# Softmax sums of a head pair inverted once per pair and multiplied into the pair's gate; masks made three tiles ahead; W_out fetched into free stream rows

## The chip, the cores and the metric

The kernel runs on one core of one Trainium2 chip. The metric is the device time of a whole execution in microseconds (us). TensorE (PE) does the matmuls, VectorE (DVE), ScalarE (ACT) and GpSimd (POOL) the rest; SyncE (SP) issues nearly all DMAs from one queue, in the order in which they stand in its program. PEld is PE's weight load, which overlaps its matmuls.

## The reference, cut to what matters

Two layers over 1024 tokens of width 1024. The change is in layer 1, whose main branch is forgetting attention (16 heads of 64 dimensions, shared keys and values, causal, with a cumulative log forget gate):

```python
logits = einsum('bqhd,bkhd->bhqk', qi, k) * scale + (cum[t] - cum[s])
p = softmax(where(kpos <= qpos, logits, -inf))
y_main = einsum('bhqk,bkhd->bqhd', p, v)
y = concatenate([y_main * silu(g_main), y_mem * silu(g_mem)])
x = layer_norm(alpha * x + y @ w_out)
```

A row of `p` is exp(..)/sum. Dividing the probabilities by the sum before the product with v, or dividing the row of `y_main` after it, gives the same. Since `y_main` is multiplied by silu(g_main), the division can also go into that gate.

## The kernel before

All large products run on PE with operands split into a high and a low half (f16 or bf16 with fp32r), so that three half-products give nearly f32 accuracy. A **slab** is a product of one 128-column piece of a weight with the whole X: 48 matmuls of 512 columns (L326). Its weights come in two pieces, each loaded (`split_w`, L210) and split into halves: by ACT (L171) and DVE (L172) before the attention stage, by POOL (L175, L192, L177) within it (`low[0]`).

The stage around the change has three parts.

- **Start** (`start_units`, L954): the values and forget logits of the first four heads (`v_first`, L835; 24 matmuls for each of eight token tiles), the key slab of pair 0 (its weights split early by `own_weights`), its query slab, and the key slab of pair 1. Between them DVE works out the forget gates in a chain of some 25 small operations (L863 to L876), whose result PE needs at L884; the cumulative sums go to DRAM (`cumd`) and come back as rows `R`, spread over the partitions (L985). The weights of the query slab and of the next key slab are split when the slab's own code is reached.
- **Attention** (`fox`, L1116): heads 0 to 15 in pairs; in each head eight query tiles, the longest first (tile 7 has 1024 keys, tile 0 has 128). For one tile, PE makes logits in one or two parts into the PSUM banks `L` (three of them); DVE adds the forget row, or on the last part the mask `C` that POOL made two tiles ahead (L978), and keeps the minimum (L1004); ACT takes exp into the PSUM banks `T` (two of them) and accumulates the sum (L1012). One tile later DVE inverts the sum (L1022 or L1024, then L1025), ACT writes the high half exp times inverse (L1040), and DVE the low half (L1041). A DMA transposes the halves (L1057); six tiles later (`LAG`) PE multiplies them with v (L1066), four tiles at a time, into the one bank `O`. ACT and DVE scale the result into `o` (L1086, L1087): for the long half two tiles after its matmuls. POOL multiplies `o` with the pair's gate (L1100), and a DMA stores it to `y1d`.
- **End** (`OutProj`, L541): W_out comes in 24 pieces of 128x512. The first ones are fetched into `land` buffers and split during pair 7; the rest through the four `raw` buffers, shared with the masks, in the last loop (`hd == HEADS`, six steps) and in `rest` (L612).

PE's order is the order of the code (`manual_schedule`); that of the other engines is set by a scheduler. Between logits and values PE works on slabs of the next pair: `Fill.pump` spreads them over a pair's 16 tiles. Each tile's share is a mean of what is left less its own attention work, so that all tiles get the same PE time; the table `MORE` then adds or takes columns by the tile's place (800 less at the first, 2330 more at the second, 1130 at the third, 1420 less at the last). A column of a 128-row operand is the unit; `VALUES` tells where the values products fall.

Of the kernel before, what the change touches and what calls it, by code (L numbers as in the profile page):

```python
# [18 lines left out]
P = 128  # L19
S = 1024  # L20
# [20 lines left out]
MORE = (-800, 2330, 1130, 410, -310, -70, -1270, -1420)  # L41
# [37 lines left out]
def trunk_kernel(ctx, tc, x, xT, memT, win, wk, wv0, wv, wmk, wmv, wout, poolw, pscale, lng, lnb, bforget, out):  # L79
# [128 lines left out]
    pinned_w = [False]  # L208

    def split_w(src_dram, shape, sc=None, r=None):  # L210
# [3 lines left out]
        if sc is not None:  # L214
            to = half_of(wt, shape)
            if low[0]:
                gp_scaled_hi_lo(to, r, sc)
            else:
                scaled_hi_lo(to, r, sc, tc.keep_in_program_order if pinned_w[0] else lambda ins: ins)
            return to  # L220
# [320 lines left out]
    class OutProj:  # L541
# [8 lines left out]
        def fetch_two(self, land):  # L550

            n = self.n + len(self.raws)
            for j in range(2):
                nc.sync.dma_start(land[:, j, :], wout[self.l, n // 2 % 2, 2 * self.KKS[n // 4] + j])
                self.raws.append(land[:, j, :])
# [56 lines left out]
        def rest(self, resid, X, dst):  # L612
# [14 lines left out]
            for sp, c in order:  # L627
# [5 lines left out]
                if splits:  # L633
                    self.split(splits.pop(0))
# [158 lines left out]
    with tc.tile_pool(name="in1", bufs=1) as in1:  # L793
# [41 lines left out]
        def v_first():  # L835
# [3 lines left out]
            for s in range(ST):  # L839
# [16 lines left out]
                )  # L856

# [52 lines left out]
        own_ws = []  # L910

        def own_weights():
            own_ws.extend(split_w(wk[0, pc], [P, 4, P], sws[1]) for pc in range(2))

        def k_units(p):
# [8 lines left out]
            yield from slab(wk[p] if p else own_ws, X, evac, g=1)  # L924
            pairs[p] = [[(own[:, 0], own[:, 1]), (odd[:, 0], odd[:, 1])]]

        def q_units(p):
# [8 lines left out]
            yield from slab(win[1, p], X, evac, g=1)  # L936
# [17 lines left out]
        def start_units(own, following):  # L954

            pinned_w[0] = True
# [32 lines left out]

# [38 lines left out]
        joined = []  # L1028

        def halves(hd, i, es, r):  # L1030

            L = (i + 1) * P
            if i in (2, 0):
                pair = joined.pop()[:, 2 * L + 2 * P :]
            else:
                pair = sb([P, 2 * S], "P", 4, F16)
                if i in (3, 1):
                    joined.append(pair)
            for lo, up, e in es:
                nc.scalar.activation(pair[:, lo:up], e, AF.Copy, scale=r)  # L1040
                nc.vector.scalar_tensor_tensor(pair[:, L + lo : L + up], e, r, pair[:, lo:up], ALU.mult, ALU.subtract)  # L1041
            return hd, i, pair
# [16 lines left out]
        def values(hd, c, o, gs):  # L1059
# [23 lines left out]

            def out():

                nc.scalar.activation(oc, acc[other, :], AF.Copy, scale=un[own])  # L1086
                nc.vector.scalar_tensor_tensor(oc, acc[own, :], un[own], oc, ALU.mult, ALU.add)  # L1087
                if b:
                    pair_out(hd // 2, c, o, gs.get(hd // 2))

            return out
# [24 lines left out]
        def fox(following, out_proj):  # L1116
            fill, past, fresh = Fill(), [None] * LAG, [None]
            gs, outs = {}, []
# [6 lines left out]
            for i in range(2):  # L1125
                mask(0, ST - 1 - i, ahead_R)
            for hd in range(HEADS + 1):
# [16 lines left out]
                for i in range(ST if hd < HEADS else LAG):  # L1144
# [4 lines left out]
                    if hd < HEADS:  # L1149
# [131 lines left out]
```

## Time and profile before

| | |
|---|---|
| median of 3 runs | 1198.69 us (1197.19 to 1199.53) |
| the profiled execution | 1197.8 us, its span 1196.0 us |
| granted TensorE clock, mean | 0.995 |
| layer 0 and the memory attention of layer 1 | 0 to about 590 us |
| start (v_first, first slabs, forget gates) | about 590 to 650 us |
| attention, 16 heads | about 650 to 1046 us |
| end (last loop, first products with W_out) | about 1046 to 1076 us |
| products with W_out and layer norm | about 1076 to 1196 us |

The span is the time from the first to the last instruction of one execution; 1.8 us of the execution's own time lie around it. A row of the timeline reads: start, duration, engine, line, operation, out<-in, shapes, count, and in brackets the idle time of the engine before it and what ended it.

### The profile page before, as it was taken

How to read it: one execution, taken by the hardware profiler on the slowest of the kernel's cores; microseconds unless marked ns; L12 is line 12 of the kernel's file. 1: busy time of each engine (PE TensorE's matmuls, PEld its weight loads, DVE VectorE, ACT ScalarE, POOL GpSimd, SP SyncE). 2: the span in 40 equal slices, each digit the busy share in tenths (PEclk: the TensorE clock that was granted, in tenths of full speed). 3: DMA queues.
4: the chain of work that ended last, by engine and by line, in shares of the span. 5: the costliest groups of instructions: out<-in, count | busy, mean ns of one | idle time of the engine just before them, and what ended most of it. 6: DMA issues, size and time to landing. Idle time of an engine off the chain costs nothing. (4 is left out here: it accounts for less than half of the span.)

```text
span 1196.0 us, 19806 instructions
## 1 busy us (share of the span) xinstructions
PE 1167.2 (98%) x6941; PEld 672.0 (56%) x6941; DVE 786.4 (66%) x1840; ACT 690.0 (58%) x1520; POOL 279.8 (23%) x429
## 2 busy tenths in 40 slices
PE   8999999999999999999999999999999999989996
PEld 5566776555555556556664555555555555445553
DVE  6744675555765557457644888778777887864654
ACT  6568875976563234466422777667766777675210
POOL 4321001310000000010324454554434331730000
PEclk8999999999999999999999999999999999999999
DMA  7576657754285555355724989979897898795430
GB/s 269 167 236 194 167 107 211 245 178 150 90 296 159 142 141 133 96 150 113 222 83 120 193 170 214 208 175 185 191 196 151 159 177 168 197 253 195 164 118 36
DMA packets 286195, 203.88 MB, mean 170 GB/s; under 512 B 224912, under 2 KB 238352, under 8 KB 286096
## 3 DMA queue, kind: packets, MB, share of 16 engines
q1 hardware_dynamic: 279696, 181.59, 60.5%
q0 software_dynamic: 6400, 21.04, 5.6%
q8 instruction: 54, 0.88, 0.3%
q14 instruction: 45, 0.37, 0.1%
HBM read 116.01 MB, written 22.61 MB: 116 GB/s over the span
## 5 line engine op out<-in xcount | busy, mean ns | idle before, releaser
L356 PE MATMUL pj<-A,w 128*128 128x512 f16 (+2 forms) x2896 | 665.1, 383 | 5.6 <-ACT w L171 2.6
L356 PEld LDWEIGHTS <-w 128*128 128x128 f16 (+1 forms) x2560 | 245.1, 98 | 280.7 <-issue 9.5
L1012 ACT ACTIVATE T<-MK,s 128x512 f32<-128x512 f32 x192 | 111.1, 579 | 62.3 <-DVE s L1004 43.0
L1041 DVE SCALAR_TENSOR_TENSOR P<-T,s,P 128x512 f16<-128x512 f32 x192 | 111.6, 613 | 41.4 <-ACT P L1040 39.1
L1040 ACT ACTIVATE P<-T,s 128x512 f16<-128x512 f32 x192 | 102.9, 576 | 55.9 <-issue 23.4
L175 POOL TENSOR_SCALAR B<-B,scales 128x512 f32<-128x512 f32 x54 | 38.8, 728 | 367.3 <-DMA B<-in_win_dram 343.5
L596 PEld LDWEIGHTS <-T 128*128 128x128 bf16 x736 | 70.6, 98 | 91.8 <-issue 7.6
L978 POOL TENSOR_SCALAR_AFFINE_SELECT raw<-R 128x256 f32<-128x256 f32 (+3 forms) x128 | 60.2, 473 | 146.4 <-DVE s L1025 72.9
L198 DVE TENSOR_TENSOR w<-raw,w 128x512 bf16<-128x512 f32 x76 | 54.3, 714 | 54.2 <-ACT w L197 38.1
L324 PE MATMUL L<-A 128*128 128x512 f16 (+3 forms) x384 | 84.5, 326 | 3.5 <-DVE s L1004 3.5
L356 PEld LDWEIGHTS pj<-A,w 128*128 128x128 f32 x352 | 65.3, 188 | 17.1 <-ACT w L197 1.3
L198 DVE TENSOR_TENSOR T<-T,T 128x1024 bf16<-128x1024 f32 x23 | 28.1, 1220 | 67.2 <-PE pj L596 37.6
L324 PEld LDWEIGHTS <-A 128*128 128x128 f16 x384 | 37.5, 98 | 48.3 <-issue 5.5
L177 POOL TENSOR_TENSOR w<-B,w 128x512 f16<-128x512 f32 x54 | 63.3, 1174 | 2.8
L197 ACT CAST w<-raw 128x512 fp32r<-128x512 f32 x78 | 48.0, 615 | 22.8 <-DMA raw<-in_win_dram 9.7
L197 ACT CAST T<-T 128x1024 fp32r<-128x1024 f32 x23 | 24.1, 1047 | 59.7 <-DMA T<-y1d 31.9
L1066 PEld LDWEIGHTS <-V 128*64 128x64 f16 (+1 forms) x1152 | 50.6, 104 | 13.9 <-issue 6.1
L1066 PE MATMUL O<-T,V 128*64 128x128 f16 (+1 forms) x1152 | 57.5, 220 | 0.5 <-DMA T<-P 0.5
L596 PE MATMUL pj<-B,T 128*128 128x512 bf16 (+1 forms) x192 | 53.2, 385 | 0.0
L199 ACT CAST w<-raw 128x512 bf16<-128x512 f32 x80 | 49.4, 618 | 5.5 <-PE pj L356 4.1
L1004 DVE CUSTOM_DVE_ANT_0 MK<-L,R,scales 128x512 f32<-128x512 f32 x64 | 45.4, 709 | 4.7 <-PE L L324 4.6
L596 PE MATMUL L<-B,T 128*128 128x512 bf16 (+1 forms) x168 | 47.3, 394 | 0.8 <-ACT T L199 0.8
(276 smaller groups left out, 1805.8 us busy)
## 6 DMA issues: line engine op xcount, KB each, us to landing
raw<-in_win_dram SPq DMA_DIRECT2D x66, 256.0 KB, 3.6
W<-in_win_dram POOLq DMA_DIRECT2D x48, 256.0 KB, 4.0
raw<-in_wout_dram SPq DMA_DIRECT2D x40, 256.0 KB, 3.2
R<-cumd SPq DMA_DIRECT2D x16, 512.0 KB, 4.6
B<-in_win_dram SPq DMA_DIRECT2D x15, 512.0 KB, 4.8
y0d<-Y SPq DMA_DIRECT2D x12, 512.0 KB, 4.2
T<-y0d SPq DMA_DIRECT2D x12, 512.0 KB, 4.5
A<-A SPq DMA_DIRECT2D x24, 256.0 KB, 4.4
```

Of the source, the lines that this page charges most:

```text
L177: nc.gpsimd.tensor_tensor(to.lo, src, to.hi, ALU.subtract)
L197: pin(nc.scalar.copy(to.hi, src))
L198: pin(nc.vector.tensor_tensor(to.lo, src, to.hi.bitcast(F32), ALU.subtract))
L199: pin((top or nc.scalar.copy)(to.top, src))
L324: nc.tensor.matmul(acc, a, b, start=i == 0, stop=i == len(terms) - 1)
L356: nc.tensor.matmul(accs[n], a[:, k, :], b[:, pc * 4 + k, n * NH : (n + 1) * NH], start=seen[n] == 1, stop=seen[n] == 3 * KT,)
L596: nc.tensor.matmul(accs[a][nh], y, w, start=kt == 8 and i == 0, stop=kt == 7 and i == 2,)
L978: nc.gpsimd.affine_select(C[:, :w], R[:, lo:up], [[-1, w]], ALU.is_ge, -NEG, base=w - P, channel_multiplier=1,)
L1012: nc.scalar.activation(e, p[:, lo:up], AF.Exp, bias=top, scale=-1.0, accum_out=sums[:, n, hd % 2, i : i + 1],)
L1040: nc.scalar.activation(pair[:, lo:up], e, AF.Copy, scale=r)
L1041: nc.vector.scalar_tensor_tensor(pair[:, L + lo : L + up], e, r, pair[:, lo:up], ALU.mult, ALU.subtract)
L1066: nc.tensor.matmul(acc[rows, (i % 4) * P : (i % 4) * P + P], v[:, b, 2 * j : 2 * j + (1 if e else 2), :].rearrange("p e d -> p (e d)"), pt ...
```

## The change

Five edits, all in layer 1.

1. **Inverse sums.** For pairs 0 to 6 the probabilities are no longer multiplied by the inverse of their sum, but by the constant `PSCALE`; ACT does so in the same step as exp (`high_halves`), DVE's low half still comes one tile later (`low_halves`). When a pair is through, DVE adds the two parts of its 16 columns of sums and inverts them (`inverse_columns`); PE transposes them, DVE copies the result out, a DMA stores it to DRAM (`invd`) and two DMAs spread it over the partitions as `I` (`inverse_rows`). POOL multiplies `I` into the pair's gate in four pieces at the sixth tile of the next pair; for pairs 3, 5 and 6, whose gate comes later, `I` itself takes the gate's place. Pair 7 stays as it was.
2. **Output.** ACT and DVE scale the values out of `O` in the step of their matmuls; POOL's products with the gate wait until both halves of the pair are there (pair 7 excepted).
3. **Masks** are made three tiles ahead, and the next head's forget rows are loaded one tile earlier.
4. **W_out** goes through free rows of the stream buffer that held keys and queries (`two_lines`), 16 pieces are split by the end of the last loop, and POOL makes their third part there too.
5. **First weights.** The weights of pair 0's queries are split during `v_first` (after tiles 3 and 5), those of pair 1's keys right after the first part of the forget gates. The table `MORE` and its use are gone, so that a tile gets the same number of slab and values columns whatever its own logits take.

```diff
-MORE = (-800, 2330, 1130, 410, -310, -70, -1270, -1420)
...
+                if s in (3, 5):
+                    next_weights(("q", 0), win[1, 0, s // 4])
...
+        def next_weights(what, src):
+            ready[what].append(split_w(src, [P, 4, P], sws[1], pin=tc.keep_in_program_order))
...
+            for pc in range(2):
+                next_weights(("k", 1), wk[1, pc])
             yield from islice(own, 58)
...
-            for lo, up, e in es:
-                nc.scalar.activation(pair[:, lo:up], e, AF.Copy, scale=r)
+            return pair
+
+        def low_halves(i, es, r, pair):
+            L = (i + 1) * P
+            for lo, up, e in es:
                 nc.vector.scalar_tensor_tensor(pair[:, L + lo : L + up], e, r, pair[:, lo:up], ALU.mult, ALU.subtract)
...
+        def inverse_columns(sums):
+            nc.vector.tensor_tensor(sums[:, 0, :, 4:], sums[:, 0, :, 4:], sums[:, 1, :, 4:], ALU.add)
+            nc.vector.reciprocal(sums[:, 0], sums[:, 0])
+
+        def inverse_rows(pr, sums):
+            t = ps([P, NH], "L", 3)[: 2 * ST, :P]
+            nc.tensor.transpose(t, sums[:, 0].rearrange("p b i -> p (b i)"), ident)
+            rows = land([P, P])[: 2 * ST]
+            nc.vector.tensor_copy(rows, t)
+            nc.sync.dma_start(invd[2 * pr : 2 * pr + 2].rearrange("h (s q) -> (h s) q", s=ST), rows)
+            I = land([P, S])
+            for b in range(2):
+                nc.sync.dma_start(I[64 * b : 64 * b + 64], invd[2 * pr + b].partition_broadcast(64))
+            return I
...
-            for i in range(2):
+            for i in range(3):
                 mask(0, ST - 1 - i, ahead_R)
...
-                    if hd < HEADS:
-                        for n, k in enumerate(range(at + i, min(last, HEADS * ST))):
-                            todo[n] += 2 * P * (ST - k % ST) - MORE[k % ST]
...
+                        if step in (3, 5, 8, 10, 12, 14):
+                            out_proj.fetch_two(two_lines({3: 0, 5: 2, 8: 4, 10: 6, 12: 0, 14: 2}[step]))
...
+                        if pr < 7:
+                            es = fresh[0][2]
+                            fresh[0] = hd, tile_of, es, PSCALE, high_halves(tile_of, es, PSCALE)
+                        if b == 0 and pr:
+                            if i == 0:
+                                inverse_columns(whole)
+                            if i == 1:
+                                I = inverse_rows(pr - 1, whole)
+                            if i == 5:
+                                g = gs.get(pr - 1)
+                                for k in range(4) if g is not None else ():
+                                    cols = slice(k * 2 * P, (k + 1) * 2 * P)
+                                    nc.gpsimd.tensor_tensor(g[:, cols], g[:, cols], I[:, cols], ALU.mult)
+                                gs[pr - 1] = I if g is None else g
...
+                        out_proj.split(11 + i, True, gp_copy)
+                        if i > 1:
+                            out_proj.fetch_two(two_lines(4 + 2 * i))
...
-                        outs.append([2 if older[1] else 0, values(older[0], older[1] // 4, older[2], gs)])
...
+                        values(older[0], older[1] // 4, older[2])
```

How the change moves instructions is shown at three places. The first is ACT in the start, from the last tiles of `v_first` on. `V` are the values of the first pairs, `G` the forget gates, `A` the keys and queries, and `w<-raw` the splits of weights. Before:

```order
L852 ACTIVATE V_5896<-pj_6107 128x2x64
L865 ACTIVATE G_5892<-G_5892 128x128
L907 ACTIVATE A_3341<-pj_6165 128x512
L171 ACTIVATE w_6197<-raw_6195,scales 128x512
L171 ACTIVATE w_6215<-raw_6213,scales 128x512
L907 ACTIVATE A_3341<-pj_6200 128x512
L907 ACTIVATE A_3341<-pj_6232 128x512
L171 ACTIVATE w_6278<-raw_6276,scales 128x512
L171 ACTIVATE w_6296<-raw_6294,scales 128x512
```

With the change, from the end of the fourth tile of `v_first` on:

```order
L170 ACTIVATE w_6020<-raw_6018,scales 128x512
L849 ACTIVATE V_5896<-pj_6023 128x2x64
...
L170 ACTIVATE w_6085<-raw_6083,scales 128x512
...
L864 ACTIVATE G_5893<-G_5893 128x128
L170 ACTIVATE w_6178<-raw_6176,scales 128x512
L170 ACTIVATE w_6183<-raw_6181,scales 128x512
L906 ACTIVATE A_3341<-pj_6186 128x512
L906 ACTIVATE A_3341<-pj_6216 128x512
```

All four splits have moved ahead of the first slab's result (`A`), which the first two used to follow directly and the last two by three results. DVE's halves of them have moved with them: the first two now stand ahead of the chain of the gates, the last two behind it.

The second place is DVE at the start of pair 3's first head. `MK<-L` is L1004 in its parts (with `R` the first, with `raw` the masked one), `P<-T` the low half, `s` and `sums` the sums and their inverse. Before:

```order
L1004 ISA MK_8552,s_8553<-L_8554,R_8286,scales 128x512
...
L1004 ISA MK_8552,s_8553<-L_8561,raw_8479,s_8553,scales 128x512
...
L1004 ISA MK_8594,s_8595<-L_8596,R_8286,scales 128x512
...
L1004 ISA MK_8594,s_8595<-L_8603,raw_8513,s_8595,scales 128x384
...
L1022 TENSOR_SCALAR s_8600<-sums_8547 128x1
L1025 RECIPROCAL s_8600<-s_8600 128x1
L1041 SCALAR_TENSOR_TENSOR P_8607<-T_8567,s_8600,P_8607 128x512
L1041 SCALAR_TENSOR_TENSOR P_8607<-T_8569,s_8600,P_8607 128x512
```

With the change:

```order
L1052 RECIPROCAL sums_7668<-sums_7668 128x16
L1046 SCALAR_TENSOR_TENSOR P_8389<-T_8420,P_8389 128x128
L1003 ISA MK_8445,s_8446<-L_8447,R_8117,scales 128x512
...
L1003 ISA MK_8445,s_8446<-L_8451,raw_8325,s_8446,scales 128x512
...
L1003 ISA MK_8493,s_8494<-L_8495,R_8117,scales 128x512
...
L1058 COPY B_8514<-L_8512 16x128
L1003 ISA MK_8493,s_8494<-L_8499,raw_8376,s_8494,scales 128x384
...
L1046 SCALAR_TENSOR_TENSOR P_8460<-T_8456,P_8460 128x512
L1046 SCALAR_TENSOR_TENSOR P_8460<-T_8458,P_8460 128x512
```

The sum and its inverse between the second tile's minima and the first tile's low halves are gone; one inversion of 16 columns stands ahead of the head, and the copy of the transposed sums between the two parts of the second tile.

The third place is SP's queue at the start of a pair with the change (it had no such rows before); `T<-P` are the transposing DMAs of probabilities:

```order
L1080 DMA_TRANSPOSE T_9237<-P_9168 128x16x128
L1059 DMA invd<-B_9229 16x128
L1062 DMA B_9232<-invd 64x1024 x2
L1080 DMA_TRANSPOSE T_9327<-P_9224 128x14x128
L1080 DMA_TRANSPOSE T_9366<-P_9316 128x12x128
```

The store and the two loads of the inverses stand between two transposes; the loads read what the store wrote.

More of the change, by code (lines that the diff above doesn't have):

```diff
@@ L1082, in values @@
             oc = o[own, c * NH : (c + 1) * NH]
[L1084 to L1091, printed above, removed]
+            nc.scalar.activation(oc, acc[other, :], AF.Copy, scale=un[own])
+            nc.vector.scalar_tensor_tensor(oc, acc[own, :], un[own], oc, ALU.mult, ALU.add)
         bfb = const.tile([P, HEADS], F32, name="bfb")
@@ L1117, in fox, with two_lines @@
             fill, past, fresh = Fill(), [None] * LAG, [None]
-            gs, outs = {}, []
+            gs = {}
+            def two_lines(row):
+                return [lines[0][:, row + j, :].bitcast(F32) for j in range(2)]
             def gate_ahead(pr):
```

71 lines of the change are left out of this document (35 added, 36 removed).

## The prediction

> **What bounds the kernel now.** I read the page's first lines, then the busy time by stage (engine: busy us and instructions; then granted clock, DMA share, GB/s).
>
> ```profile
> span 1196.0 us, 19806 instructions
> PE 1167.2 (98%) x6941; PEld 672.0 (56%) x6941; DVE 786.4 (66%) x1840; ACT 690.0 (58%) x1520; POOL 279.8 (23%) x429
> 590.00:650.00 60.00, 54.97 (x385) 35.51 (x384) 31.20 (x70) 11.81 (x30) 16.87 (x24) 1.00 0.44 142
> 650.00:1046.00 396.00, 392.52 (x2747) 206.50 (x2746) 313.08 (x910) 276.46 (x659) 186.94 (x287) 1.00 0.88 181
> 1046.00:1076.00 30.00, 26.04 (x173) 13.77 (x172) 18.82 (x32) 21.58 (x39) 11.11 (x13) 1.00 0.94 249
> ```
>
> PE is the bound in every stage: over the span it idles 28.8 us, in the attention 3.5 of 396. The change removes no matmul and touches no work before 590 us or after 1076 us. So it can win only PE's idle time in the three stages between: 5.0 + 3.5 + 4.0 = 12.5 us. PE's waits in these windows say for what (us in total, times, longest):
>
> ```profile
> PE pj L356 <- ACT w L171: 2.6, 2, 1.3
> PE pj L356 <- DVE w L172: 1.7, 1, 1.7
> PE L L324 <- DVE s L1004: 3.5, 6, 1.1
> PE L L596 <- DVE w L198: 1.4, 1, 1.4
> PE pj L596 <- DVE MK L198: 1.0, 2, 0.7
> PE L L596 <- ACT T L199: 0.8, 1, 0.8
> PE O L1066 <- DMA T<-P: 0.5, 1, 0.5
> ```
>
> The first two rows are the start (weights split too late), the third is the attention (a PSUM bank that DVE has not read yet), the last four are the end.
>
> **The start.** PE stops three times, each time for a half of slab weights; the rows of the timeline:
>
> ```profile
> 597.21 0.84 SPq L213 DMA_DIRECT2D raw<-in_win_dram  x2
> 618.91 5.34 PE L356 MATMUL pj<-A,w 128*128 128x512 f16 x24
> 620.52 0.23 DVE L863 TENSOR_SCALAR G<-G 128x128 f32<-128x128 f32 x1
> 625.55 1.90 PE L356 MATMUL pj<-A,w 128*128 128x512 f16 x8 [1.30 <-ACT w L171]
> 628.37 0.75 DVE L172 SCALAR_TENSOR_TENSOR w<-raw,scales,w 128x512 f16<-128x512 f32 x1
> 629.18 5.79 PE L356 MATMUL pj<-A,w 128*128 128x512 f16 x26 [1.73 <-DVE w L172]
> 631.66 0.29 DVE L876 TENSOR_TENSOR G<-G 128x128 f32<-128x128 f32 x1
> 634.80 0.38 PE L884 MATMUL O<-G,G 128*128 128x128 f32 x2
> 641.09 10.53 PE L356 MATMUL pj<-A,w 128*128 128x512 f16 x48 [1.30 <-ACT w L171]
> ```
>
> The weights were issued at 597, long landed; only the order on ACT and DVE keeps the splits late. Moved ahead, they fall in `v_first`, where ACT is busy 12 us in 60 and DVE 31: all 4.3 us go. What is late next is the chain of the forget gates. It runs on DVE from 620.5 to 632.0 with two of these splits in it (0.75 each); without them it ends at 630.5. PE starts the slabs at 618.9 and has 24 + 34 matmuls, 58 times 0.219 (10.53 over 48), before L884: 631.6. One us is left, so I take -4.3, with -2.3 as the other end, should the chain slip by 3 us.
>
> **The attention.** Group rows of the engines that PE waits for (busy us, mean ns, then idle before):
>
> ```profile
> L1004 DVE CUSTOM_DVE_ANT_0 MK<-L,R,scales 128x512 f32<-128x512 f32 x64 | 45.4, 709 | 4.7 <-PE L L324 4.6
> L1004 DVE CUSTOM_DVE_ANT_0 MK<-L,raw,s 128x512 f32<-128x512 f32 (+1 forms) x64 | 41.0, 640 | 3.9 <-DVE s L1004 1.1 <-PE O L1066 0.9 <-POOL raw L978 0.7
> L1012 ACT ACTIVATE T<-MK,s 128x512 f32<-128x512 f32 x192 | 111.1, 579 | 62.3 <-DVE s L1004 43.0 <-DVE P L1041 18.9
> L1041 DVE SCALAR_TENSOR_TENSOR P<-T,s,P 128x512 f16<-128x512 f32 x192 | 111.6, 613 | 41.4 <-ACT P L1040 39.1
> L1022 DVE TENSOR_SCALAR s<-sums 128x1 f32<-128x1 f32 x64 | 13.5, 210 | 13.7 <-ACT T L1012 13.3
> L1024 DVE TENSOR_SCALAR s<-sums 128x1 f32<-128x1 f32 x64 | 9.6, 150 | 10.0 <-ACT T L1012 9.5
> L1025 DVE RECIPROCAL s<-s 128x1 f32<-128x1 f32 x128 | 20.7, 162 | 2.8
> L1087 DVE SCALAR_TENSOR_TENSOR G<-O,scales,G 64x512 f32<-64x512 f32 x32 | 24.0, 750 | 11.4 <-ACT G L1086 10.6
> L908 DVE SCALAR_TENSOR_TENSOR A<-pj,A 128x512 f16<-128x512 f32 x32 | 21.8, 683 | 7.1 <-ACT A L907 6.9
> L1066 PE MATMUL O<-T,V 128*64 128x128 f16 (+1 forms) x1152 | 57.5, 220 | 0.5 <-DMA T<-P 0.5
> ```
>
> The inverse goes for 112 of 128 tiles: 7/8 of 13.5 + 9.6 + 20.7 is 38 us off DVE, whose share falls from 79% (313 of 396) to about 69%. DVE is not the bound, so this is worth nothing by itself; what counts is latency. In each tile exp, sum, inverse, high half, low half stood in one chain, and the low half frees the `T` bank for the next exp (18.9 us of ACT's idle time before exp are this wait, `DVE P L1041`). With the change the high half follows exp on ACT at once.
>
> Against it works the loss of `MORE`. A tile's PE time in a middle pair is 144 matmuls of 0.219 over 16 tiles (1.97), the values 57.5/128 (0.45), and the logits, 0.11 for each 128 keys: 2.42 + 0.88 = 3.30 for the first tile, 3.19 for the second, down to 2.53. Before, it was their mean, 2.91, with `MORE`: 2.57, 3.91, 3.39, 3.09, down to 2.30. DVE's work in the second tile is its minima (0.71 + 0.64 + 0.1), the low halves of a full tile (1.4), the output that is no longer put off (0.75) and a share of slab results (0.26): 4.1 us against 3.19, so DVE falls 0.9 us behind there, and 1.4 + 1.25 + 0.26 = 2.9 against 3.08 in the third tile holds it. By the same count the kernel before lost most in its fourth tile (3.6 against 3.09). How much lag is free? The second part of the second tile takes the bank of the first part of the first tile:
>
> ```profile
> 969.05 1.03 PE L324 MATMUL L<-A 128*128 128x512 f16 x4
> 972.08 0.74 DVE L1004 CUSTOM_DVE_ANT_0 MK<-L,R,scales 128x512 f32<-128x512 f32 x1
> 972.89 0.48 PE L324 MATMUL L<-A 128*128 128x384 f16 x2 [0.66 <-DVE s L1004]
> ```
>
> Here the logits began at 969.05, DVE read them only at 972.08, and PE, there again after 2.6 us, waited. Five of the six waits stand at this place. The change gives it 3.30 - 2.57 = 0.73 us more room and an earlier low half in front of it. Waits of 0.2 to 0.7 then vanish; the longest, 1.1, shrinks. I take -2.5 of 3.5, with ends at -3.5 and 0.
>
> Added on PE are seven transposes, each in front of the second tile's slab work. The nearest row is the one transpose of the start; the others price the way of the inverses:
>
> ```profile
> 638.44 0.27 PE L892 MATMUL T<-ident,G 128*128 128x128 f32 x1
> cumd<-G SPq DMA_DIRECT2D x1, 64.0 KB, 1.5
> R<-cumd SPq DMA_DIRECT2D x16, 512.0 KB, 4.6
> L1100 POOL TENSOR_TENSOR G<-G,G 128x256 f32<-128x256 f32 x20 | 16.0, 821 | 20.7 <-DVE G L1087 20.7
> ```
>
> Seven times 0.27 is 1.9 us, 0 if they fall into waits; pipelined, I take 0.2 each, +1.4. The copy and the inversion of the columns, three small DVE operations (L1022 and L1025 took 0.21 and 0.16), replace 16 tiles' sums and cost nothing. Store and load land after 1.5 + 4.6 = 6.1 us, plus some 4 us into the pair until the copy: 10 us, four tiles, and they are used at the sixth. POOL gets 16 more products of 0.82 (13 us in 396, where it is busy 187); the masks behind them have three tiles, about 9 us, against 3.3 us for four products. All this is hidden; what it costs if it is not stands with the rivals.
>
> **The end.** The pieces of W_out come late (from the chain of waits, and the timeline):
>
> ```profile
> 1060.87 5.40 DMA raw<-in_wout_dram
> 1064.25 1.05 ACT L197 CAST T<-T 128x1024 fp32r<-128x1024 f32 x1 [2.90 <-DMA T<-y1d]
> ```
>
> The chain waits 5.4 us for a load of W_out; then ACT and DVE split four pieces while PE waits 1.0 + 1.4. With the change the pieces up to 16 are fetched and split before, and the eight later ones have two groups of 48 matmuls, 21 us, as cover. So -2.4. The 0.8 us for y stays, since `T<-y1d` still waits for a buffer and lands late, and so does the 0.5 for the last transpose. Ends: -3.7 and 0.
>
> **Sum**, against the profiled execution (span 1196.0 and 1.8 us around it, 1197.8): -4.3 - 2.5 + 1.4 - 2.4 = -7.8, so 1190.0. The median of the runs is 0.9 above that execution: **1190.9 us**. By all favourable ends (-4.3 - 3.5 + 0 - 3.7) it is 1187.2, by all unfavourable ones (-2.3 + 0 + 1.9 + 0) 1198.3.
>
> **Rivals.** (1) *Slower: DVE's lag outgrows the banks.* Place: the second tile of each head. From about 2.3 us of lag (3.30 until PE is back, plus 0.4 for its first part, less 0.4 for the logits and 0.8 and 0.2 for DVE to read them) every head stalls. For it: 4.1 us of work against 3.19, the output no longer put off, and in seven pairs a transpose that takes a third bank there and is copied out between the minima. Against it: 0.9 is far from 2.3, and the chain is shorter. Price: the longest wait seen, 1.1, in 16 heads, 17.6, in place of -2.5: 1211.
>
> (2) *About the same: the way through DRAM blocks SP.* SP's loads of `I` wait for the store's landing, and transposes wait behind. If each of the seven pairs lost one landing of 1.5 us at PE's values, 10.5 us would be added: 1201; with part of it hidden, 1198. Against it: PE waits for a transpose once in 128 tiles now, and they have six tiles of room. The Trainium skill, in "DMA: Bandwidth & Descriptors", section "Anatomy of one DMA", puts most of a transfer's fixed 2 us on the receipt of the write, heaviest for HBM; by it seven landings would be an estimated 14 us, and the time 1205 if none were hidden. The row of `cumd` shows 1.5 us here.
>
> (3) *A part does not do what it says:* the end stays as it is, since the last loop is bound by ACT and the late y. 1193.3.
>
> The Trainium skill has one more rule against the change, in "SBUF — State Buffer", section "Who interferes with whom": a DVE instruction with two SBUF inputs is blocked for the whole of a GpSimd instruction that reads SBUF. The 16 new POOL products would meet it; but DVE's attention work reads PSUM in its first operand, so by it rival 1 gains little, and I leave its chance as it is.
>
> **Chances.** Forecast 0.55, rival 1 0.20, rival 2 0.15, rival 3 0.10. The forecast's own range is 1187 to 1198. The whole range reaches into rivals 1 and 2: **1186 to 1203**; above lies most of rival 1 and the skill's end of rival 2. About 0.2%, 2.4 us, is what a measurement tells from no change here, so faster means under 1196.3. Faster: 0.53 of the forecast, all of 3 and a little of 2, 0.66; same 0.13; slower 0.21.
>
> **What would show it.** Right: no PE wait on `w` between 620 and 645, L884 within 0.5 us of its last slab matmul; PE's wait on L1003 under 2 us in total; no wait on W_out pieces after the last loop, the wait on y still there; the attention some 1 us shorter. Rival 1 would show as waits of `L` on DVE, once a head, over 10 us together; rival 2 as waits of `O` on the transposes early in each pair. The forecast is wrong if PE's idle time from 590 to 1076 us is above 8 us, or if the time changes outside that window.

## The result, and the profile after

The changed kernel takes **1234.38 us** (median of 5 runs, 1231.98 to 1236.05) against 1197.89 us for the kernel before (1197.19 to 1199.53): a ratio of 1.030, 95% interval 1.0277 to 1.0323, 36.5 us slower. The forecast was 1190.9, its range ended at 1203. The profiled execution took 1234.5 us.

The page's first lines, then the busy time by stage (columns as before):

```profile
span 1232.7 us, 19655 instructions
PE 1178.9 (96%) x6948; PEld 675.2 (55%) x6948; DVE 753.2 (61%) x1637; ACT 670.3 (54%) x1512; POOL 301.5 (24%) x465
590.00:650.00 60.00, 59.86 (x409) 38.21 (x407) 31.65 (x77) 14.25 (x36) 13.48 (x19) 1.00 0.32 97
645.00:1092.00 447.00, 409.39 (x2771) 211.63 (x2770) 290.77 (x723) 266.52 (x672) 215.70 (x333) 0.95 0.88 187
1092.00:1122.00 30.00, 30.00 (x193) 18.64 (x192) 17.86 (x23) 19.57 (x33) 11.47 (x12) 1.00 0.69 202
```

The stages have moved: the attention now runs from 645 to 1092 us, and the end follows. The start gained what was forecast and a little more: PE idles 0.1 us there instead of 5.0. In the end PE has no idle time, instead of 4.0 us. In the attention DVE is relieved (from 79% to 65% of the stage), but PE now idles 37.6 us instead of 3.5. PE's waits between 590 and 1100 us say for what:

```profile
PE L L321 <- DMA A<-A: 26.1, 3, 9.6
PE L L321 <- issue: 4.4, 1, 4.4
PE L L321 <- DVE s L1003: 4.3, 2, 3.8
PE pj L353 <- POOL w L191: 2.8, 1, 2.8
```

The six small waits on DVE's minima are down to one of 0.5 us; the 3.8 us and the 2.8 us on POOL's split fall into the last pair, at 1070 and 1055 us, where W_out is split beside the attention. In place of the small waits stand four long ones, at the first logits of pairs 2, 4, 6 and 7; the three that are named wait for the `A<-A` moves, the last step in which the next pair's queries are made (`move` in `q_units`). The first of them in PE's timeline:

```profile
731.32 2.54 PE L353 MATMUL pj<-A,w 128*128 128x512 f16 x11
743.14 1.86 PE L321 MATMUL L<-A 128*128 128x512 f16 x4 [9.29 <-DMA A<-A]
```

Why the moves came late is read from the two queues that stand ahead of them, SP's and POOL's. SP's queue in that stretch (start and duration of the issue; a space between two rows is SP waiting):

```profile
708.17 0.42 SPq L330 DMA_DIRECT2D B<-in_win_dram  x1
715.28 0.32 SPq L1118 DMA_DIRECT2D y1d<-G  x1
715.70 1.20 SPq L903 DMA_DIRECT2D A<-A  x2
716.99 5.29 SPq L1080 DMA_TRANSPOSE T<-P  x2
...
722.96 0.58 SPq L330 DMA_DIRECT2D B<-in_wk_dram  x1
723.65 5.77 SPq L1080 DMA_TRANSPOSE T<-P  x2
735.49 0.33 SPq L988 DMA_DIRECT2D R<-cumd  x1
735.87 1.11 SPq L903 DMA_DIRECT2D A<-A  x2
...
740.21 0.51 SPq L903 DMA_DIRECT2D A<-A  x1
```

And POOL's timeline:

```profile
703.94 2.78 POOL L1215 TENSOR_TENSOR G<-G,B 128x256 f32<-128x256 f32 x4 [3.64 <-DMA B<-invd]
...
708.64 1.36 POOL L174 TENSOR_SCALAR B<-B,scales 128x512 f32<-128x512 f32 x2
...
710.44 1.20 POOL L191 TENSOR_SCALAR w<-B 128x512 f16<-128x512 f32 x2
711.61 2.27 POOL L176 TENSOR_TENSOR w<-B,w 128x512 f16<-128x512 f32 x2
713.84 1.41 POOL L1116 TENSOR_TENSOR G<-G,G 128x256 f32<-128x256 f32 x2
...
727.82 1.36 POOL L174 TENSOR_SCALAR B<-B,scales 128x512 f32<-128x512 f32 x2 [9.47 <-DMA B<-in_wk_dram]
729.14 1.20 POOL L191 TENSOR_SCALAR w<-B 128x512 f16<-128x512 f32 x2
730.31 2.27 POOL L176 TENSOR_TENSOR w<-B,w 128x512 f16<-128x512 f32 x2
...
735.18 0.29 POOL L981 TENSOR_SCALAR_AFFINE_SELECT raw<-R 128x128 f32<-128x128 f32 x1
```

The two queues wait for each other in turn. SP stands 6.7 us before the store of pair 0's output (708.6 to 715.28), until POOL's products are made, which stood behind I and, after it, behind a split of weights (708.64 to 713.84). The load of the next key weights, behind that store, goes out at 722.96. POOL reaches the first step of their split at 718.3 and waits 9.5 us for them, with masks behind. The last of these masks reads the forget rows whose buffer SP's load of `R` needs, so SP stands until 735.49, and the queries' moves stand behind `R`. SP's waits for POOL between 650 and 1046 us, in total:

```profile
SPq L988 <- POOL raw L981: 27.9, 7, 6.3
SPq L1118 <- POOL raw L981: 24.8, 6, 6.9
```

The Trainium skill, in "DMA: Bandwidth & Descriptors", section "Anatomy of one DMA", says that a semaphore wait of a DMA takes place on the issuing sequencer, before dispatch. The rows at 715.28 and 735.49 agree: while one DMA waits, the next in the list isn't issued.

The stall costs more than its idle time. The busy time of three stretches around it (the number after POOL's is the granted clock):

```profile
727.00:737.00 10.00, 6.85 (x50) 3.43 (x47) 4.66 (x13) 5.38 (x15) 9.18 (x13) 1.00 0.53 104
737.10:747.40 10.30, 4.26 (x11) 1.50 (x12) 2.09 (x5) 1.17 (x4) 1.82 (x5) 0.50 1.02 208
747.40:757.00 9.60, 9.60 (x89) 5.61 (x88) 6.03 (x15) 5.53 (x13) 0.90 (x2) 1.00 0.72 111
```

3.3 us into the idle time the clock falls to half and stays there for 10.2 us, 4.2 of them after PE has work again, where a matmul of 512 columns starts every 427 ns instead of every 216, so 2.1 us are lost beside the 9.3. The kernel before has no such stretch between 590 and 1190 us, the changed one six; after PE's return they hold 26 us at half clock, 13 us lost.

So the account of the profiled executions is: attention idle +34.1 (37.6 against 3.5), low clock in these stages +13, seven transposes +1.9, end -4.0, start -4.9: +40, where +36.7 was measured. Of the 3 us between, 1.4 lie outside these stages, where the kernel before lost 3.1 us to the low clock and the changed one 1.7; the rest I could not place.

The 3.8 us in the last pair come from an engine that the chain above leaves out. DVE, just ahead of the minima that PE waits for:

```profile
1066.66 5.73 DVE L197 TENSOR_TENSOR MK<-A,MK 128x512 bf16<-128x512 f32 x1
```

This is DVE's step in a split of W_out; its median is 0.68 us. It began during an instruction of POOL, ran through eight more that followed without a pause, and ended 0.54 us after the last of them. In the profiled execution twelve such steps began during an instruction of POOL between 560 and 1150 us; eleven ended 0.54 to 0.57 us after the end of one (the twelfth, of twice the columns, 1.07). So DVE's step seems to have stood until POOL was through. The longest of the six waits before the change, 1.1 us at 1024.7, stands behind such a step too (1.69 us). No run takes POOL's work away at this place, so this reading rests on the times alone.

### The profile page after: what moved, and what is told of

Its sections match the earlier page's. It is cut to its first block, busy times and chain, and to the rows that moved or that the text cites. A ratio compares the mean times of both kernels' runs of the same rounds, so it can differ in the third digit from the quotient of the medians.

```text
span 1232.7 us, 19655 instructions
## 1 busy us (share of the span) xinstructions
PE 1178.9 (96%) x6948; PEld 675.2 (55%) x6948; DVE 753.2 (61%) x1637; ACT 670.3 (54%) x1512; POOL 301.5 (24%) x465
## 5 line engine op out<-in xcount | busy, mean ns | idle before, releaser
L353 PE MATMUL pj<-A,w 128*128 128x512 f16 (+2 forms) x2896 | 672.5, 387 | 4.1 <-POOL w L191 2.8
L353 PEld LDWEIGHTS <-w 128*128 128x128 f16 (+1 forms) x2560 | 248.1, 99 | 288.6 <-issue 23.1
L174 POOL TENSOR_SCALAR B<-B,scales 128x512 f32<-128x512 f32 x54 | 38.4, 720 | 380.2 <-DMA B<-in_win_dram 337.5
L1046 DVE SCALAR_TENSOR_TENSOR P<-T,P 128x384 f16<-128x384 f32 (+1 forms) x168 | 90.6, 554 | 50.6 <-ACT P L1039 49.5
L1003 DVE CUSTOM_DVE_ANT_0 MK<-L,R,scales 128x512 f32<-128x512 f32 x64 | 45.7, 714 | 72.5 <-PE L L321 68.4
L1039 ACT ACTIVATE P<-T 128x384 f16<-128x384 f32 (+1 forms) x168 | 74.9, 478 | 12.0 <-DMA T<-P 10.6
L176 POOL TENSOR_TENSOR w<-B,w 128x512 f16<-128x512 f32 x54 | 61.9, 1155 | 0.8
```

Of the source, the lines that this page charges most:

```text
L176: nc.gpsimd.tensor_tensor(to.lo, src, to.hi, ALU.subtract)
L353: nc.tensor.matmul(accs[n], a[:, k, :], b[:, pc * 4 + k, n * NH : (n + 1) * NH], start=seen[n] == 1, stop=seen[n] == 3 * KT,)
```

## The experiments

Each run's own comparison with the kernel before is given, since the median of the kernel before moved between 1196.2 and 1198.9 from one set of runs to the next. Times are medians; the interval is that of the ratio.

**First: which link of the chain.** Theory Q said that the order of SP's queue does it, theory W that POOL has too much work. Four variants of the changed kernel:

```diff
# e1 (the store), e2 (the loads of R), e3 (both)
-                nc.sync.dma_start(y1d[pr // 4, :, pr % 4, :], o)
+                nc.gpsimd.dma_start(y1d[pr // 4, :, pr % 4, :], o)
-            nc.sync.dma_start(R, cumd[hd].partition_broadcast(P))
+            nc.gpsimd.dma_start(R, cumd[hd].partition_broadcast(P))
# e4
-                                for k in range(4) if g is not None else ():
+                                for k in ():
```

> The changed kernel with one edit: the store of a pair's finished output (y1d<-G, L1118) is issued by POOL, which made its last product, and no longer by SP. Theory Q (queue): in the changed kernel SP stands 6.9 us at this store waiting for POOL's products; the load of the next key weights behind it goes out late, POOL waits 9.5 us for that load, its masks come late, SP then waits 6.1 us to load the next rows of forget gates, and the moves of the next pair's queries stand behind that load, so PE waits 9.3, 9.6, 7.2 and 4.4 us at the starts of pairs 2, 4, 6 and 7. By Q the whole chain falls with the store: the waits of PE for the moves (26.1 + 4.4 us) go to under 4 us, POOL's wait for the key weights goes under 3 us, and the time falls by 30 us and more, to 1192 to 1204. Rival W (work): POOL simply has too much to do and is late whatever queue the store is on; then PE's waits stay over 20 us and the time stays over 1222.

Measured: 1227.5 us, ratio 1.0226 (1.0191 to 1.0262). Neither theory: 7 us of 36 came back (9 by the ratios). The key weights still went out at 720.8 behind two transposes, and POOL still waited 7.7 us for them.

> The changed kernel with one edit: the loads of the forget gates' rows (R<-cumd, L988) are issued by POOL and not by SP. By theory Q this takes out the last link alone: the store still blocks SP for about 7 us and POOL still waits for the key weights, but the moves of the queries no longer wait for R's buffer. In the changed kernel they went at 735.9 and 740.2 in pair 1, after a wait of 6.1 us; they would go about 6 us earlier, so PE's waits shrink from 9.3, 9.6, 7.2 and 4.4 to about 3, 3, 1 and 0 us and the time to 1203 to 1215. By rival W the masks and weights of POOL are what is late, POOL has 16 more instructions in front of them, and the time is the same or longer, over 1228.

Measured: 1210.6 us, ratio 1.0109 (1.0048 to 1.0169), as Q has it. PE's waits of this run:

```profile
PE L L321 <- issue: 13.4, 3, 8.3
PE L L321 <- ACT MK L810: 2.8, 1, 2.8
```

Pairs 2, 4 and 6 are down to 2.8, 2.8 and 2.3 us; pair 7 waits longer than before the edit, 8.3. So in the changed kernel R's load ahead of the moves is the last link, shown.

> The changed kernel with both edits, the store of a pair's output and the loads of R issued by POOL. By theory Q nothing on SP is left that waits for POOL ahead of the queries' moves: PE waits under 2 us for moves, time 1190 to 1202, at most 3 us from the run with the store alone. By rival W still over 1222.

Measured: 1214.5 us, ratio 1.0128 (1.0094 to 1.0162). No better than e2; Q's figure is missed.

> The changed kernel without the four products of a gate with its inverses (L1215, 16 on POOL in all); the inverses of pairs 0, 1, 2 and 4 are then left out of the output. Both theories expect a gain here, but of different size. Theory Q: the products with the output no longer stand behind 3.6 us of waiting for the inverses and 2.8 us of products, the store is reached 6.4 us earlier, so SP's wait at it (6.9) all but goes for pairs 0, 1, 2 and 4, and with it the chain: 1193 to 1207. Rival W: only the work itself goes, 4 times 2.8 us = 11 us: 1222 to 1226.

Measured: 1231.9 us, ratio 1.0272 (1.0223 to 1.0320). Both missed: without the 16 products next to nothing changes. (POOL's 12 products of the outputs of pairs 3, 5 and 6 with I, which the kernel before doesn't have either, are still there.) In its POOL timeline the wait for the key weights is still 9.3 us. Something else makes POOL's weight work late, with or without more work for POOL.

**Second: what bunches POOL's weight work.** The order of POOL's instructions in the changed kernel for head 3 (R1102 is its row buffer; B1246 and B1247 are the weights of pair 3's queries and keys; L174, L191 and L176 are the three steps of a split):

```
120 L981 AFFINE_SELECT raw1177_7368<-R1102_7008 128x512
121 L981 AFFINE_SELECT raw1187_7449<-R1102_7008 128x384
122 L174 TENSOR_SCALAR B1247_7696<-B1247_7696,scales_108 128x512 x2
123 L191 TENSOR_SCALAR w1248_7698<-B1247_7696 128x512
124 L191 TENSOR_SCALAR w1251_7717<-B1247_7696 128x512
125 L176 TENSOR_TENSOR w1248_7698<-B1247_7696,w1248_7698 128x512
126 L176 TENSOR_TENSOR w1251_7717<-B1247_7696,w1251_7717 128x512
127 L981 AFFINE_SELECT raw1196_7484<-R1102_7008 128x256
```

The traces show the same, by the split steps that stand between the masks of one head and those of the next: of 120 in heads 2 to 13 of the changed kernel, 2 stand in even heads, in the kernel before 48 of 102. In e1 to e4 the counts by head are the changed kernel's, even without the products. In e6 (below), where the inverses are taken out, 50 of 102 stand in even heads. How far POOL is ahead shows at 705 us, counted in half slabs (a slab's weights come in two pieces). The kernel before has made the first step of 32 of them and the second of 12, so it is 20 ahead; the changed kernel has made 10 and 10. `rows` and `I` come from `land`, the ring of ten buffers (tag B) into which the slabs' weights are loaded, each in its turn. SP's DMAs of that ring in the changed kernel from 579.86 to 701.27 us are these alone:

```profile
579.86 0.42 SPq L330 DMA_DIRECT2D B<-in_wk_dram  x1
692.61 0.34 SPq L1059 DMA_DIRECT2D invd<-B  x1
697.32 1.18 SPq L1062 DMA_DIRECT2D B<-invd  x2
701.27 1.07 SPq L330 DMA_DIRECT2D B<-in_wv_dram  x1
```

The kernel before loads the weights of six slabs between 643 and 698 us. That the loads stand behind I, since it takes its turn in the ring, is theory B. Four runs:

```diff
# e5: rows and I in two free rows of the tile of queries and keys
-            rows = land([P, P])[: 2 * ST]
+            I = [lines[0][:, row, :].bitcast(F32) for row in (7, 15)]
+            rows = I[0][: 2 * ST, :P]
...
-            I = land([P, S])
             for b in range(2):
-                nc.sync.dma_start(I[64 * b : 64 * b + 64], invd[2 * pr + b].partition_broadcast(64))
+                for h, to in enumerate(I):
+                    nc.sync.dma_start(to[64 * b : 64 * b + 64], invd[2 * pr + b, h * NH : h * NH + NH].partition_broadcast(64))
# e6: each tile's inverse as before
-                        if fresh[0] and fresh[0][0] >= HEADS - 2:
+                        if fresh[0]:
-                        if pr < 7:
+                        if False:
-                        if b == 0 and pr:
+                        if False:
# e7: in the kernel before
+                    if i == 1 and b == 0 and 0 < pr < 8:
+                        for n in range(2):
+                            nc.vector.tensor_copy(land([P, P])[:, :8], whole[:, 0, 0, :])
...
# e8: in the kernel before, the diff's next_weights and its calls
```

> The changed kernel with one edit: the inverses' rows and the spread inverses I lie in two rows of the tile of queries and keys that no pair uses, and no longer in the ring of ten buffers that the slabs' weights are loaded into (tag B); I is loaded in four pieces instead of two. After the first four runs: the products and the store explain 7 us at most, the loads of R on SP 24 us. New theory B (ring): because I and its rows take their turn in the ring of weights, no weights of a later slab are loaded or split before I's turn; in the changed kernel's order POOL has no weight work in the even heads and all of it in the odd ones, each split right behind its load, so it stands up to 9.8 us for a load with the masks behind it. With I out of the ring the order has the splits spread over both heads and the loads far ahead again. By B POOL's waits for the loads of weights, 40 us in the changed kernel, go under 8, PE's waits for the queries' moves (26.1 + 4.4) under 4, and the time is 1187 to 1198. Rival D (the way through DRAM): store, loads and products of I themselves keep SP and POOL late wherever I lies; they are all still there, with two more loads a pair: over 1215.

Measured: **1204.1 us**, ratio 1.0060 (1.0040 to 1.0080). 29 of the 36.5 us came back by moving two buffers, more than rival D allows and somewhat less than B forecast. POOL is 20 half slabs ahead at 705 us again, and PE's waits for the moves fell from 30.5 us to 6.6, where B had said under 4:

```profile
PE L L321 <- issue: 6.0, 2, 3.0
PE pj L353 <- POOL w L191: 1.7, 1, 1.7
PE L L321 <- DMA A<-A: 0.6, 1, 0.6
```

B's other figure is wrong: POOL's waits for weights did not go under 8 us. They are 68 us in this run, more than the 45 of the changed kernel:

```profile
POOL B L174 <- DMA B<-in_win_dram: 35.7, 7, 8.7
POOL B L174 <- DMA B<-in_wv_dram: 17.2, 4, 4.9
POOL B L174 <- DMA B<-in_wk_dram: 15.5, 3, 9.4
```

What differs is what stands behind such a wait. In the changed kernel nine steps of splits stood between the end of the wait and the last mask (727.82 to 735.18); here it is six (724.67 to 730.48), since the rest was done in the even head, and R's load goes at 730.8 instead of 735.5.

> The changed kernel with each tile's inverse multiplied into its probabilities again, as before the change (no sums by pair, no transposes of inverses, no way through DRAM, no products of gate and inverse); the masks three ahead, the weights of the start, the pair's output and W_out as the change has them. Theories B and D both expect the loss to go: PE's waits for moves under 3 us, the time 1187 to 1197. If it stays over 1215, neither holds and the loss comes from the other edits (masks and R's loads, MORE). What it gains against the kernel before is what those other edits are worth: by the prediction's terms -4.3 at the start and -2.4 at the end, with up to 3.5 us of waits on DVE for the banks still there.

Measured: 1193.3 us, ratio 0.9972 (0.9957 to 0.9986), faster than the kernel before. The loss comes with edit 1; masks three ahead, R's earlier load and the later output cost nothing that can be seen. The waits on DVE that edit 1 had removed are back:

```profile
PE L L321 <- DVE s L1003: 5.1, 7, 1.6
```

> The kernel before with nothing of the change, but two buffers of the ring of weights taken at the second tile of each even head from the second pair on, each written by a copy of 8 columns of the last pair's sums on DVE (14 such copies, together some 3 us of DVE) and read by nothing. Theory B: this alone makes weights' loads and splits bunch (the order shows 4 slabs' first products together at the end of an odd head) and so makes POOL and SP late: slower than before by 4 to 30 us, with PE waiting for moves or weights in most pairs. Rival D, or any theory by which the ring is innocent: within 2 us of the kernel before.

Measured: 1201.9 us, ratio 1.0031 (1.0009 to 1.0053): 3.7 us slower, 1 to 6 by the interval, so it decides neither for B's least, 4, nor for the rival's 2. PE's waits are short ones on DVE, not on moves. POOL's first steps bunch in the odd heads here too, but the other steps don't (40 of 114 in even heads), and at 705 us POOL is still 4 half slabs ahead: the next loads go out at 673.5 us, not at 701.3. So taking a place in the ring isn't enough by itself. In the changed kernel the place is also held until the pair's sums are there and have gone through DRAM. POOL's products with I aren't what holds it: e4 has none of them in the pairs with a gate, and its next load goes out at 706.1 us. No run holds the place longer and changes nothing else, so this part of B is argued and not shown.

> The kernel before with one edit of the change alone: the weights of the queries of pair 0 and the keys of pair 1 are loaded and split during the values at the start. The changed kernel's trace has 0.1 us of PE idle time between 590 and 650 against 5.0 before. If this is a gain by itself the time is 4 to 5 us under the kernel before, about 1193.5; rival: the slabs done earlier are only waited for later (L banks, DVE), and the gain is under 2 us.

Measured: 1193.6 us, ratio 0.9976 (0.9958 to 0.9994). The start's gain is real and stays; at 2.9 us (0.7 to 5.0 by the interval) it lies between theory and rival.

**Third: what is left in e5.**

```diff
# e9: e5 with R's loads issued by POOL; e11: e9 with MORE; e10: e6 with MORE
-            nc.sync.dma_start(R, cumd[hd].partition_broadcast(P))
+            nc.gpsimd.dma_start(R, cumd[hd].partition_broadcast(P))
# e12: e5, POOL doesn't use I
-                                for k in range(4) if g is not None else ():
+                                for k in ():
-                                gs[pr - 1] = I if g is None else g
+                                pass
# e13: e12 without the way through DRAM
-                            if i == 1:
-                                I = inverse_rows(pr - 1, whole)
# e14: e5 with e1's edit; e15, e16: e5 with the store and loads of I on nc.gpsimd, nc.scalar
```

> The run with I in its own rows (1204.1) and, beside it, the loads of R issued by POOL. In that run PE still waits 3.0 and 2.9 us at the starts of pairs 2 and 4: SP stands at R's load (issued at 730.80, behind a mask of POOL's) with the queries' moves (731.18, 735.44) behind it, the same last link as in the changed kernel. Theory Q for what is left: with R off SP these two waits go under 1 us together, with them the low clock behind them, and the time is 1192 to 1199. Rival W for what is left: the loads cost POOL more than they free on SP (in the first four runs both on POOL was no better than one), and the time is 1202 or more.

Measured: 1208.2 us, ratio 1.0086 (1.0065 to 1.0108): Q fell here. Its SP queue shows another DMA in R's old place, a load of weights whose buffer POOL frees at 736.4, with the moves again behind it, and PE waiting until 746.1:

```profile
736.48 0.38 SPq L330 DMA_DIRECT2D B<-in_win_dram  x1
736.92 1.10 SPq L903 DMA_DIRECT2D A<-A  x2
...
742.11 0.46 SPq L903 DMA_DIRECT2D A<-A  x1
```

> The changed kernel with each tile's inverse in its probabilities again (1193.3) and with the table MORE of slab work by tile restored as well. Without MORE PE waits 5.1 us in 7 places for DVE's minima (L1003) at the second tiles of heads, the kernel before 3.5 in 6. Theory: MORE is worth 1 to 2 us by these waits, so PE's wait on L1003 falls under 3.5 and the time is 1190.5 to 1192.5. Rival: MORE is worth nothing, 1193 and more.

Measured: 1194.6 us, ratio 0.9972 (0.9956 to 0.9987). PE's wait on L1003 fell to 2.9 us in 6 places as expected; the time did not, so `MORE` is worth nothing that these runs can tell.

> The changed kernel with I in its own rows, R's loads issued by POOL, and MORE restored. It tells what the inverse by pairs is worth once its way is clear: against the run with the sums back and MORE, PE's waits on DVE's minima (some 3 us) should be gone, seven transposes are added. The prediction's terms give -2.5 + 1.4, about 1 us less than that run: 1189 to 1192. Rival: POOL's 16 products, the stores and the loads cost more than the waits on DVE gave, and the time is 1194 or more.

Measured: 1211.5 us, ratio 1.0102 (1.0084 to 1.0120). The rival holds.

> The run with I in its own rows, and POOL makes no product with I (16 products fewer; the gates and, in the pairs without a gate in time, the outputs stay without the inverses, which are left out of the output). Store and loads of I still run. Theory P (POOL's line): POOL, in order, waits 9 + 15 us for I in the attention and spends 2.8 us a gated pair on the products; that makes the output's store, SP's wait at it, the next weights and R late. Then the time goes from 1204 to 1192 to 1198, and PE's waits at the starts of pairs 2 and 4 (3.0 and 2.9 us) under 1. Theory S (SP's line): the five DMAs a pair that SP issues for I are what delays it; then the time stays over 1200.

Measured: 1199.7 us, ratio 1.0018 (1.0006 to 1.0030): 5 us less than e5 in the ratio. Theory P has a share, but not the whole.

> As the run before it, and without I altogether: no transpose of the inverses, no store and no loads of I (the inverses are left out of the output). By theory S it is this run that goes to 1190 to 1196, and the one before it stays over 1200. By theory P it is within 3 us of the one before it, lower by the seven transposes (1 to 2 us). If both stay over 1200, neither is the cause, and what remains is the order that the halves and the later output take.

Measured: **1189.8 us**, ratio 0.9930 (0.9913 to 0.9947), another 10 us less. With the way gone, PE is hardly ever idle in the attention; its busy time there and its one wait:

```profile
650.00:1046.00 396.00, 395.18 (x2766) 208.31 (x2764) 284.55 (x709) 265.05 (x667) 190.08 (x292) 1.00 0.94 190
PE L L321 <- DVE s L1003: 0.8, 1, 0.8
```

> The run with I in its own rows, and the store of a pair's output issued by POOL, which makes its last product; nothing is left out. If SP's wait at this store (10.2 us in 4 places there, up to 3.2) is the link that is left, the loads of weights behind it go out some 2 to 3 us earlier, PE's two waits of 3 us at pairs 2 and 4 go under 1.5, and the time is 1194 to 1200. In the changed kernel the same edit gave 7 us of 36. If it stays within 2 us of 1204, the store is not it.

Measured: 1201.6 us, ratio 1.0029 (1.0015 to 1.0043): 3.7 us less than e5 by the ratios, short of the forecast.

> The run with I in its own rows (1204.1), with the store and the four loads of I issued by POOL instead of SP; nothing is left out. If SP's line is what costs the 10 us of the way, and POOL, which has to wait for I anyway, can take it, the time is 1193 to 1198. If the transfers or transposes cost them, or POOL's own line is as tight as SP's (five more issues a pair, each followed by masks and weights), it stays at 1201 or more.

Measured: 1219.8 us, ratio 1.0185 (1.0147 to 1.0224). SP's wait for POOL at R's load is back at 39.2 us in 7 places: POOL, which waits 20.6 us in those pairs for the store's landing, makes its masks late.

> The same with ACT issuing the store and the loads; a tile's exponentials and high halves lie between store and loads in ACT's order, so ACT waits less for the store's landing. If SP's line is the cost: 1192 to 1197, PE's waits for moves and transposes gone. Against it: ACT waits for DVE's copy and for the store with exponentials behind it; if that weighs more, PE waits on L or T banks for ACT, and the time is 1200 or more.

Measured: 1222.1 us, ratio 1.0197 (1.0147 to 1.0246). Both lose: on SP, where the change put it, the way through DRAM is cheapest. Whether its 10 us there come from SP's waits, from the transfers or from the transposes is not settled by these runs.

## Why the prediction was wrong

- **The step that failed** is the last one of the attention's paragraph, "All this is hidden". It priced the way of the inverses by durations (1.5 + 4.6 us of landing, 0.82 for a product) against slack in tiles. The landings were sized rightly (the store 1.7 us, the loads 4.1); of the products it counted 16, where POOL got 28, with the 12 that multiply I into the outputs of pairs 3, 5 and 6. It never asked from which buffers `rows` and `I` come, nor what stands ahead of and behind the added DMAs and products in two in-order queues that wait for each other. By ratios: 29 us of the loss were the ring (e5), 5 POOL's use of I, 28 products (e12 against e5), 10 the way itself, with the seven transposes (e13 against e12); against these stands the gain.
- **Rival 2** named the right queue at the wrong place: it had transposes waiting behind the loads of I, at 10.5 us. PE waited for moves of queries behind R's load, at the start of a pair, 4 to 10 us at a time, and for no transpose. That the way costs 10 us by e13, near its 10.5, bears it out in the number alone: how the way costs them isn't settled, so this may be luck.
- **The waits that it costed at nothing** had cover in masks "three tiles ahead". The cover was real for DVE (PE lost nothing on masks), but a mask is also the last reader of R's buffer, and R's load was ahead of the moves on SP. The user of the buffer after next was not followed.
- **The clock** was left out: none of the rivals adds anything behind a stall, and up to 13 us of the loss are half clock after one.
- **The gains were right.** Start: -4.3 forecast; 4.9 us of idle time gone, and alone it makes 0.24% or 2.9 us (e8, by its ratio). Attention: -2.5 forecast, ends 0 and -3.5; e13, which has this gain without its delivery, is 0.42 points of the ratio, 5.0 us, under e6, with PE's wait on minima 0.8 against 5.1. `MORE`'s loss, its counterweight, shows in e6's 5.1 against 3.5. All terms but the transposes sum to -9.2; e13 stands 8.4 us under the kernel before (0.70%). The forecast is the time of a kernel that has its inverses for nothing.
- **The end** (-2.4) gained more than forecast, 4.0 us, and the forecast said that the waits for y and for the last transpose would stay. But everything that the end waits for had some 40 us longer to arrive. In e13, without the loss, PE idles 1.05 us in the 30 us from 1046, 2.9 less than before, and waits there for the split of y (0.9), as forecast.
- **POOL and DVE.** The prediction set aside what POOL can do to a DVE instruction with two SBUF inputs, since DVE's attention work reads PSUM. Edit 4 puts splits of W_out beside the last pair's attention, and both inputs of DVE's step there lie in SBUF. The step of 5.73 us shown above is one of them, and PE lost 3.8 us behind it.
- **Rival 1** (DVE's lag outgrows the banks) did not occur: PE's waits on DVE's minima are two, not one a head, and the long one is the step above.

The fastest complete kernels are e6 (1193.3), e8 (1193.6) and e10 (1194.6), not told apart from one another and each some 3 us faster than the kernel before: the change without edit 1, or its first weights alone.

## What to carry to other kernels

A new buffer costs by the ring that it is taken from, not by its bytes: in a ring shared with prefetched weights it sets how far ahead the prefetch can be ordered. A cheap tile that waits for a late result seems to pull the later loads back behind that result (20 half slabs of lead against none). When an edit is costed as hidden, follow it through every in-order queue that it enters, to the next transfer behind each wait, and to the last reader that frees that transfer's buffer; the order listing of before and after shows bunching before anything runs. And price a stall of PE above about 3 us with what it does to the clock.

## What the runs showed of the hardware

In the 18 profiled executions, between 560 and 1150 us, all 29 idle times of PE of 3.0 us or more (up to 9.8) were followed by a stretch at a granted clock of 0.5. Of the 20 between 2.0 and 2.9 us 13 were, of the 50 between 0.9 and 1.9 us two (one of them just ahead of an idle time of 4.4 us). The stretches last 3.4, 6.8 or 10.2 us, never between; idle times over 7 us had 6.8 or 10.2. The Trainium skill, in "TensorE: Matmul & The Clock Gate", section "Why this matters for your kernels", asks for no idle gaps over some 3 us, since one idle window puts the array back to half rate. The runs agree, and add that 2 us can be enough. What I had not expected is the size of it here: up to a third of the loss.
